# Transposing v and y of a delta-rule recurrence in whole 128x128 pieces instead of 64x64 ones

## The chip, the cores and the metric

The kernel runs on one core of one Trainium2 chip. The metric is the device time of one execution in microseconds (us). Engines go by the names that the profile gives them: PE (matrix products), PEld (its weight loads), DVE, ACT and POOL (elementwise work), SP (which issues most transfers).

## What is computed

One transformer-like block over 2048 tokens of width 1024: a modulated input projection, a gated MLP branch, a recurrent branch, a gated merge, an output projection with a layer norm, and a feed-forward layer of 4096 hidden features with a second layer norm. All is float32. The recurrent branch is what the change touches. Cut to that, the reference reads:

```python
def step(state, inp):            # 8 heads of 64 features, one state of 64x64 for each
    rt, wt, kt, vt, at, bt = inp
    sa = jnp.einsum('bhij,bhj->bhi', state, at)
    state = state * wt[:, :, None, :] + sa[..., None] * bt[:, :, None, :] + vt[..., None] * kt[:, :, None, :]
    yt = jnp.einsum('bhij,bhj->bhi', state, rt)
    return state, yt
...
y = (y - mu) * lax.rsqrt(var + GN_EPS) * gn_gain + gn_bias      # mu, var over the 64 features of a head
return (y + bonus) * g
```

## The kernel before, in words

The 2048 tokens are taken in four blocks of 512. A product with a float32 weight is made of three float32r products of 128x512 each (`mm3`, lines 461 to 463), because every operand is split into a rounded upper part and a rest (`split`: a rounding copy on ACT at line 395, a subtraction on DVE at line 396). These products fill PE nearly all the time. They come from `fm` (tiles `fm_ps`), from the feed-forward layer (`ff`, `pf`), from the output projection (`ops`) and from `uv` (`vps`).

The recurrent branch of a block runs between these products. `weave` (line 203) takes one step of the products (six of them, mostly) and lets the branch put its next part into PE's stream after as many steps as its last `yield` asked for. PE's order is thus written out by hand (`ORDERED`); the order on DVE, ACT, POOL and SP is made by a scheduler. A block's branch goes in four groups of 128 tokens, each of two chunks of 64: 16 groups in all. `rwkv_a` prepares the factors of a group, `rwkv_b` inverts its triangular matrices, and `rwkv_c` runs the recurrence over its two chunks.

`rwkv_c` is where the change lies. The features of two heads lie on the 128 partitions: head 0 of a pair on the lower 64 (`E`), head 1 on the upper 64 (`O`); there are `NP` = 4 pairs. `zq[:, p, 2]` holds v of pair p for the 128 tokens.

- At the start, v is turned so that tokens lie on partitions. For each chunk, head and pair, one 64x64 piece goes through `turn` (line 174), onto the half of the partitions that the head doesn't occupy. A piece from the lower half is made as an ordinary product with the identity (line 180 serves `rows.start == 0`, and each such product is two instructions in the trace), one from the upper half as a transposing instruction (line 178). Per group that is 16 pieces into two PSUM tiles `vt`; for each chunk ACT copies one half into `Q[O, 0]` (line 751) and DVE the other into `Q[E, 1]` (line 752).
- Then each chunk makes the tiles `xy` and `us` (lines 769 to 790), and its output leaves `xy` by a copy on ACT (line 793) and one on DVE (line 794) into `Yt`, with each head on its own half of the partitions.
- The group norm works on `Yt` (lines 796 to 805). Eight steps of products later, pair by pair with one step between, y is turned back: four 64x64 pieces by `turn` into `yp[:, 0]`, followed by the gate's product of 96x128 (line 813, two instructions in the trace) into `yp[:, 1]`. ACT and DVE take `yp` from there (lines 815 to 817).

Of the kernel before, what the change touches and what calls it, by code (L numbers as in the profile page):

```python
# [8 lines left out]
F32 = mybir.dt.float32  # L9
# [7 lines left out]
P = 128  # L17
# [6 lines left out]
C = 64  # L24
NC = HB // C
GW = 512
RW = 512
NP = 4
# [5 lines left out]
HC = 4  # L34
ORDERED = {mybir.EngineType.PE}
# how many steps of the products each part of the work between them stays behind, and a factor for each block
# [28 lines left out]
# weight tiles fetched ahead; first FF tiles that start under the transposes, and their lag  # L65
# [3 lines left out]
# the engine (a: ACT, v: DVE) that rounds the upper parts  # L69
# [20 lines left out]
class Body:  # L90
# [15 lines left out]
    # ---------------------------------------------------------------- setup  # L106
# [67 lines left out]
    def turn(self, out, x, rows):  # L174
        """transpose onto the other half of the partitions; the transposing form writes the lower half only"""
        ident = self.ident[rows, rows]
        if rows.start:
            self.nc.tensor.transpose(out, x, ident)
        else:
            self.nc.tensor.matmul(out, lhsT=x, rhs=ident, start=True, stop=True)  # L180

# [21 lines left out]
    def weave(self, gen, bg, drain=True):  # L203
        """bg yields how many steps of gen its next part should stay behind"""
        due = 0.0
        for _ in gen:
            due -= 1.0
            while due <= 0.0:
                w = next(bg, None)
                if w is None:  # L210
                    due = 1e9
                else:
                    due += w * self.lat
        if drain:
            self.go(bg)
# [5 lines left out]
    def setup(self):  # L221
# [5 lines left out]
        # masks over (s, t): strict t > s and inclusive t >= s, on both halves of the partitions  # L227
# [16 lines left out]
        # unit columns of the forward substitution: row i of lane group q is column 4 i + q  # L244
# [7 lines left out]
        # the two heads' indicators, and ones on the two heads' blocks  # L252
# [9 lines left out]
        # per-feature constants  # L262
# [11 lines left out]
        # 1 - mu and (1 - mu) bias  # L274
# [5 lines left out]
        # state  # L280
# [6 lines left out]
        # modulation: mod = silu(c) @ w_ada + b_ada, features on partitions  # L287
# [8 lines left out]
    def spatial_bias(self, wsT, spB, ones):  # L296
        """b_ln_v times the spatial weights' sums over s, + b_spatial, features on partitions"""
# [11 lines left out]
    def first_tiles(self):  # L309
        """the first projections of block 0, input tile by input tile as their modulation arrives"""  # L310
# [21 lines left out]
    def setup2(self):  # L332
        """the rest of the modulation"""
# [5 lines left out]
        # half of gt1 (the sigmoids are kept as 1 + tanh) and gt1 * b_out, along the free axis  # L339
# [6 lines left out]
    def setup3(self):  # L346
# [7 lines left out]
        # h2 = xhat * (g1 (1+sc2)) + (b1 (1+sc2) + sh2);  residual = xhat * (alpha g1) + (alpha b1 + gt2 b_ff2)  # L354
# [8 lines left out]
    def load_silu(self, pool):  # L363
        """2 silu(c) on every partition"""
# [7 lines left out]
    def load_ws(self, wsT):  # L372
        """[s, g, t], kept where t >= s"""
# [14 lines left out]
    # ------------------------------------------------------------ helpers  # L388
    def split(self, src, hi, lo, eng=None):
        """hi = src rounded to float32r, lo = src - hi: their products carry float32's digits"""  # L390
# [7 lines left out]
    def order(self):  # L398
        """the weight tiles in the order in which the projections take them"""
# [41 lines left out]
    def weights(self, n=D):  # L441
        """the next weight tile; those after it are fetched ahead"""
# [22 lines left out]
    def fm(self, xs, m=P, kt=KT, koff=0, each=None):  # L465
        """[m features, 512 tokens] = weights^T x, x feature-major in two parts"""
# [41 lines left out]
    def shift_mix(self, ps, m, name, i, c, out):  # L508
        """out = (1 - mu) z + mu (z of the token before), z = ps + bias"""
# [36 lines left out]
    # --------------------------------------------------------------- rwkv  # L546
# [15 lines left out]
    def rwkv_a(self, b, h, q):  # L562
# [26 lines left out]
        def first(p):  # L589
# [25 lines left out]
            # a~ = -k^ P(t-1), r~ = r P;  b~ = k^ a / P, k~ = k' / P  # L615
# [12 lines left out]
        def second(p, bk, kp):  # L628
# [13 lines left out]
            # bonus: (sum over the head of r k' r_k) v  # L642
# [11 lines left out]
        # squared norms of k^, one row for each head of a pair  # L654
# [4 lines left out]
        # 32 x 32 diagonal blocks and their norms, one for each lane; each lane group q solves 8 columns  # L659
# [12 lines left out]
    def rwkv_b(self, q):  # L672
# [16 lines left out]
        # T = (1 - L)^-1 diag(rn) by forward substitution  # L689
# [43 lines left out]
    def rwkv_c(self, b, h, q):  # L733
# [9 lines left out]
        Qs = []  # L743
        for c in range(NC):
            cs = slice(c * C, c * C + C)
            Q = rp.tile([P, 2, NP, C], F32, name="Q", tag="Q", bufs=2)
            vt = pst([P, 2, NP, C], "vt")
            for i in range(2):
                for p in range(NP):
                    self.turn(vt[half[1 - i], i, p], zq[half[i], p, 2, cs], half[i])  # L750
            nc.scalar.copy(out=Q[O, 0], in_=vt[O, 0])
            nc.vector.tensor_copy(out=Q[E, 1], in_=vt[E, 1])
            Qs.append(Q)
        # chunk by chunk
        Yt = rp.tile([P, NC, NP, C], F32, name="Yt", tag="Yt")
        for c in range(NC):
# [36 lines left out]
            nc.scalar.copy(out=Yt[O, c], in_=xy[O, 0])  # L793
            nc.vector.tensor_copy(out=Yt[E, c], in_=xy[E, 1])
        # group norm over each head, tokens on partitions
        yv = Yt.rearrange("p c h i -> p (c h) i")
# [11 lines left out]
        for p in range(NP):  # L808
            yp = pst([P, 2, HB], "yp")
            for i in range(2):  # L810
                for c in range(NC):
                    self.turn(yp[half[i], 0, c * C:c * C + C], Yt[half[1 - i], c, p], half[1 - i])
# [373 lines left out]
```

## Time and profile before

| | |
|---|---|
| median of 3 runs | 3162.5 us (3161.28 to 3165.88) |
| span of the profiled execution | 3158.4 us |
| instructions in the profile | 45776 |
| PE, DVE, ACT, POOL busy | 98%, 67%, 40%, 5% of the span |
| chain that ended last | PE 88%, DVE 6%, DMA 3%, ACT 1%, issue 1% |
| mean granted clock of PE | 0.996 of full speed |

The span runs from the first to the last instruction of the profiled execution, and it is the only time that the profile has of that execution. The median of the runs is 4.1 us (0.13%) above it. A busy share is an average over stages; which engine sets the pace in a stage is read from that stage's own rows. In a timeline, a row is one instruction, or several of one kind in a row (x4: four of them), with its start and how long it took from the start of the first to the end of the last. Matmuls overlap each other on PE, so the time that PE spends on one is the distance between starts, not its duration.

### The profile page before, as it was taken

The page shows a single profiled execution, that of the slowest core. Times are in us where ns is not written, and L with a number is a line of the kernel's source. Part 1 is how long each engine was busy: PE and PEld are TensorE (multiplying, and loading weights), DVE is VectorE, ACT ScalarE, POOL GpSimd, SP SyncE. Part 2 cuts the span into 40 slices and gives each one's busy share as a digit, 9 for nine tenths or more (in the row PEclk, how much of TensorE's full clock was granted, in tenths as well). Part 3 has the DMA queues.
Part 4 walks back from the last instruction along what each step waited for, and adds up shares of the span by engine and source line. Part 5 has one row for each costly group of instructions (what it writes and reads, how often), then busy time and mean ns, then how long its engine had stood idle before and what let it go on. Part 6 is the DMA issues. An engine that isn't in the chain of part 4 may idle for free.

```text
span 3158.4 us, 45776 instructions
## 1 busy us (share of the span) xinstructions
PE 3105.3 (98%) x17072; PEld 2485.8 (79%) x17072; DVE 2126.4 (67%) x4727; ACT 1267.9 (40%) x2012; POOL 143.8 (5%) x370
## 2 busy tenths in 40 slices
PE   8999999999999999999999999999999999999998
PEld 6776778777777877878777888787877788888887
DVE  7877873778777676586676557567668655854445
ACT  5524433353433334434433343453434334253332
POOL 1101100000000000100000000110000000000000
PEclk9999999999999999999999999999999999999999
DMA  8465544823323266444232245544333234623332
GB/s 286 152 177 162 171 144 144 279 90 85 103 77 93 81 198 200 140 135 123 92 96 84 87 138 192 174 120 155 105 97 91 83 87 134 230 87 96 98 97 97
DMA packets 241487, 416.78 MB, mean 132 GB/s; under 512 B 72465, under 2 KB 127377, under 8 KB 241265
## 3 DMA queue, kind: packets, MB, share of 16 engines
q1 hardware_dynamic: 241184, 413.59, 42.4%
q8 instruction: 135, 2.21, 0.3%
q14 instruction: 88, 0.71, 0.1%
q0 software_dynamic: 80, 0.26, 0.0%
HBM read 357.60 MB, written 56.17 MB: 131 GB/s over the span
## 4 chain that ended last, share of the span: by engine, by line
PE 88%; DVE 6%; DMA 3%; ACT 1%; issue 1%; SPq 0%; POOL 0%; DVEq 0%; ACTq 0%
PE fm_ps L461 15%; PE fm_ps L463 14%; PE fm_ps L462 14%; PE ff L461 7%; PE ff L462 7%; PE ff L463 7%; PE xy L769 2%; PE ops L462 1%; PE ops L463 1%; PE ops L461 1%; PE s L633 1%; PE vps L461 1%; PE vps L463 1%; PE vps L462 1%; PE us L778 1%; PE us L784 1%
## 5 line engine op out<-in xcount | busy, mean ns | idle before, releaser
L395 ACT CAST whi<-wraw 128x1024 fp32r<-128x1024 f32 (+1 forms) x500 | 494.9, 991 | 924.2 <-PE fm_ps L462 457.7
L396 DVE TENSOR_TENSOR wlo<-wraw,whi 128x1024 fp32r<-128x1024 f32 (+1 forms) x500 | 573.6, 1149 | 355.4 <-ACT whi L395 347.1
L461 PE MATMUL fm_ps<-xh,whi 128*128 128x512 f32 x1984 | 795.7, 401 | 2.9 <-ACT xh L395 2.3
L462 PE MATMUL fm_ps<-xl,whi 128*128 128x512 f32 x1984 | 774.2, 390 | 2.8 <-DVE xl L396 2.8
L463 PE MATMUL fm_ps<-xh,wlo 128*128 128x512 f32 x1984 | 775.0, 391 | 0.6 <-DVE wlo L396 0.6
L461 PEld LDWEIGHTS fm_ps<-xh,whi 128*128 128x128 f32 x1984 | 370.6, 187 | 91.6 <-issue 4.7
L463 PEld LDWEIGHTS fm_ps<-xh,wlo 128*128 128x128 f32 x1984 | 370.6, 187 | 83.1 <-DVE wlo L396 1.4
L462 PEld LDWEIGHTS fm_ps<-xl,whi 128*128 128x128 f32 x1984 | 371.1, 187 | 78.2 <-DVE xl L396 5.5
L461 PE MATMUL ff<-hh,whi 128*128 128x512 f32 (+1 forms) x1056 | 416.1, 394 | 0.7 <-ACT hh L395 0.7
L462 PE MATMUL ff<-hl,whi 128*128 128x512 f32 (+1 forms) x1056 | 404.9, 383 | 0.3 <-DVE hl L396 0.3
L463 PE MATMUL ff<-hh,wlo 128*128 128x512 f32 (+1 forms) x1056 | 404.7, 383 | 0.0
L1063 DVE SCALAR_TENSOR_TENSOR zr<-ff,mod,zr 128x512 f32<-128x512 f32 (+1 forms) x264 | 184.8, 731 | 149.4 <-PE ff L463 149.1
L461 PEld LDWEIGHTS ff<-hh,whi 128*128 128x128 f32 x1056 | 198.6, 188 | 45.4 <-issue 6.0
L463 PEld LDWEIGHTS ff<-hh,wlo 128*128 128x128 f32 x1056 | 198.5, 188 | 39.9
L462 PEld LDWEIGHTS ff<-hl,whi 128*128 128x128 f32 x1056 | 198.7, 188 | 35.8 <-DVE hl L396 0.5
L695 DVE TENSOR_TENSOR tmp<-T,L 128x4 f32<-128x4 f32 (+23 forms) x496 | 162.5, 328 | 10.4
L696 DVE TENSOR_REDUCE T<-tmp 128x1 f32<-128x4 f32 (+23 forms) x496 | 123.5, 249 | 10.3
L396 DVE TENSOR_TENSOR hl<-r,hh 128x512 fp32r<-128x512 f32 x128 | 87.9, 689 | 49.0 <-ACT hh L395 48.9
L462 PE MATMUL ops<-wlo,mh 128*128 128x512 f32 x256 | 101.2, 395 | 4.1 <-DVE wlo L396 4.1
L461 PE MATMUL ops<-whi,mh 128*128 128x512 f32 x256 | 101.3, 396 | 2.3 <-DVE ga L926 1.8
L462 PE MATMUL fm_ps<-yl,whi 128*128 128x512 f32 x256 | 102.1, 399 | 1.0 <-DVE yl L396 1.0
L461 PE MATMUL fm_ps<-yh,whi 128*128 128x512 f32 x256 | 102.7, 401 | 0.2 <-ACT yh L395 0.2
(240 smaller groups left out, 4099.9 us busy)
## 6 DMA issues: line engine op xcount, KB each, us to landing
wraw<-in_w_ff_dram SPq DMA_DIRECT2D x260, 512.0 KB
wraw<-in_w_gate_dram SPq DMA_DIRECT2D x64, 512.0 KB
wada<-in_w_ada_dram SPq DMA_DIRECT2D x48, 512.0 KB
wraw<-in_w_rkv_dram SPq DMA_DIRECT2D x42, 512.0 KB
gd<-g SPq DMA_DIRECT2D x64, 256.0 KB
ga<-gd SPq DMA_DIRECT2D x64, 256.0 KB
wraw<-in_w_out_dram SPq DMA_DIRECT2D x32, 512.0 KB
zd<-zmix SPq DMA_DIRECT2D x48, 256.0 KB
```

Of the source, the lines that this page charges most:

```text
L395: nc.scalar.copy(out=hi, in_=src)
L396: nc.vector.tensor_sub(lo, src, hi.bitcast(F32))
L461: nc.tensor.matmul(ps, lhsT=wh, rhs=xh, start=start, stop=False)
L462: nc.tensor.matmul(ps, lhsT=wh, rhs=xl, start=False, stop=False)
L463: nc.tensor.matmul(ps, lhsT=wl, rhs=xh, start=False, stop=stop)
L633: nc.tensor.matmul(sc[:, c], lhsT=bk[half[i], c], rhs=G[i][half[i], p, c], start=True, stop=True)
L695: nc.vector.tensor_mul(tmp[:, :n, :w], T[:, :n, :w], L[:, :w, t][:, None, :].to_broadcast([P, n, w]))
L696: nc.vector.tensor_reduce(T[:, :n, t:t + 1], tmp[:, :n, :w], axis=AX.X, op=ALU.add)
L769: nc.tensor.matmul(xy[:, i, p], lhsT=G[i][:, p, c], rhs=Q[:, i, p], start=(i == 0 and p == 0), stop=False, skip_group_check=True)
L778: nc.tensor.matmul(us[r, 0, p], lhsT=TT[r, p * NC + c], rhs=Xs[r, p], start=True, stop=True)
L784: nc.tensor.matmul(us[half[i], 1, p], lhsT=BK[:, p, c, half[i]], rhs=Q[:, i, p], start=True, stop=True)
L1063: self.nc.vector.scalar_tensor_tensor(res[:, n, ts], pfs[i], self.mod[:, 40 + n:41 + n], res[:, n, ts], op0=ALU.mult, op1=ALU.add)
```

## The change

For each group, v of a pair is turned in one transposing instruction of 128x128 instead of four pieces of 64x64. The result holds both chunks on the two halves of the partitions and both heads side by side, in one tile `vt` instead of two. The copies out of it, still two per chunk and of 64x256 elements each, take chunk c from its half and write the half where `Q` wants it, so for some the partitions that are read are not those that are written. `Yt` is laid out in the same way: token on the partitions, the two heads of a pair side by side; the copies out of `xy` write the half of their chunk, in four stretches of 64 elements. Then y of a pair is turned back by one transposing instruction of 128x128. `turn` is gone. The group norm, the gate's product, all other products, the DMAs and the numbers in the `yield`s stay. (The rest of the diff takes comments out.)

```diff
-        Qs = []
-        for c in range(NC):
-            cs = slice(c * C, c * C + C)
-            Q = rp.tile([P, 2, NP, C], F32, name="Q", tag="Q", bufs=2)
-            vt = pst([P, 2, NP, C], "vt")
-            for i in range(2):
-                for p in range(NP):
-                    self.turn(vt[half[1 - i], i, p], zq[half[i], p, 2, cs], half[i])
-            nc.scalar.copy(out=Q[O, 0], in_=vt[O, 0])
-            nc.vector.tensor_copy(out=Q[E, 1], in_=vt[E, 1])
-            Qs.append(Q)
-        Yt = rp.tile([P, NC, NP, C], F32, name="Yt", tag="Yt")
+        vt = pst([P, NP, 2, C], "vt")
+        for p in range(NP):
+            nc.tensor.transpose(vt[:, p], zq[:, p, 2], self.ident)
+        Qs = [rp.tile([P, 2, NP, C], F32, name="Q", tag="Q", bufs=2) for c in range(NC)]
+        for c in range(NC):
+            nc.scalar.copy(out=Qs[c][O, 0], in_=vt[half[c], :, 0])
+            nc.vector.tensor_copy(out=Qs[c][E, 1], in_=vt[half[c], :, 1])
+        Yt = rp.tile([P, NP, 2, C], F32, name="Yt", tag="Yt")
...
-            nc.scalar.copy(out=Yt[O, c], in_=xy[O, 0])
-            nc.vector.tensor_copy(out=Yt[E, c], in_=xy[E, 1])
-        yv = Yt.rearrange("p c h i -> p (c h) i")
+            nc.scalar.copy(out=Yt[half[c], :, 0], in_=xy[O, 0])
+            nc.vector.tensor_copy(out=Yt[half[c], :, 1], in_=xy[E, 1])
+        yv = Yt.rearrange("p k h i -> p (k h) i")
...
             yp = pst([P, 2, HB], "yp")
-            for i in range(2):
-                for c in range(NC):
-                    self.turn(yp[half[i], 0, c * C:c * C + C], Yt[half[1 - i], c, p], half[1 - i])
+            nc.tensor.transpose(yp[:, 0], Yt[:, p], self.ident)
             nc.tensor.matmul(yp[:, 1], lhsT=self.gup[:, p * P:p * P + P], rhs=xg, start=True, stop=True)
```

How the instructions stand on PE where v of the first group is turned, between the products of block 0's gates, before the change:

```order
L463 MATMUL fm_ps<-xh_153,wlo 128x512
L180 MATMUL vt<-ident,zq 64x64 x4
L178 MATMUL vt<-ident,zq 64x64 x4
L180 MATMUL vt<-ident,zq 64x64 x4
L178 MATMUL vt<-ident,zq 64x64 x4
L461 MATMUL fm_ps<-xh_154,whi 128x512
L462 MATMUL fm_ps<-xl_162,whi 128x512
```

And with it (lines have moved up by 8 here, and by 12 at the end of `rwkv_c`):

```order
L455 MATMUL fm_ps<-xh_153,wlo 128x512
L738 MATMUL vt<-ident,zq 128x128 x4
L453 MATMUL fm_ps<-xh_154,whi 128x512
L454 MATMUL fm_ps<-xl_162,whi 128x512
L455 MATMUL fm_ps<-xh_154,wlo 128x512
```

Sixteen pieces of two kinds have become four instructions of one kind, between the same two products.

On PE where y of the first pair of the first group is turned back, before:

```order
L463 MATMUL fm_ps<-xh_155,wlo 128x512
L178 MATMUL yp<-ident,Yt 64x64 x2
L180 MATMUL yp<-ident,Yt 64x64 x2
L813 MATMUL yp<-xg,gup 128x128
L461 MATMUL fm_ps<-xh_148,whi 128x512
L462 MATMUL fm_ps<-xl_156,whi 128x512
```

And with the change:

```order
L455 MATMUL fm_ps<-xh_155,wlo 128x512
L800 MATMUL yp<-ident,Yt 128x128
L801 MATMUL yp<-xg,gup 128x128
L453 MATMUL fm_ps<-xh_148,whi 128x512
L454 MATMUL fm_ps<-xl_156,whi 128x512
```

Four pieces have become one instruction, before the same product of the gate. The rest of PE's order is the same, instruction for instruction. On DVE, ACT, POOL and SP the scheduler has exchanged some neighbours, and no kind of instruction has become more or fewer.

On ACT, the copies out of `vt` of the first group wait for other engines as follows, before (a name in brackets is the engine that is waited for):

```order
L729 COPY TT<-tps 32x8x32 [waits DVE_49]
L751 COPY Q<-vt 64x256 [waits PE_49] x2
L891 ACTIVATE g<-fm_ps,hv 128x512 [waits DMAHW0_49,PE_49,Activation_49]
```

And with the change:

```order
L721 COPY TT<-tps 32x8x32 [waits DVE_49]
L741 COPY Q<-vt 64x256 [waits PE_49]
L741 COPY Q<-vt 64x256 [waits DVE_49]
L879 ACTIVATE g<-fm_ps,hv 128x512 [waits DMAHW0_49,PE_49,Activation_49]
```

The second copy on ACT, which waited for PE, now waits for DVE's copy out of the same tile.

## Rows read from the trace of the kernel before

**Rows 1.** The page, part 1: busy time, share of the span, instructions of an engine.

```profile
PE 3105.3 (98%) x17072; PEld 2485.8 (79%) x17072; DVE 2126.4 (67%) x4727; ACT 1267.9 (40%) x2012; POOL 143.8 (5%) x370
```

**Rows 2.** The page, part 4: the chain that ended last, by engine.

```profile
PE 88%; DVE 6%; DMA 3%; ACT 1%; issue 1%; SPq 0%; POOL 0%; DVEq 0%; ACTq 0%
```

**Rows 3.** Waits on PE, longest and one other: us in total, times, longest.

```profile
PE first L461 <- ACT xh L395: 12.9, 1, 12.9
...
PE yp L178 <- DVE Yt L805: 1.2, 1, 1.2
```

**Rows 4.** Windows A:B: length, busy time by engine, PE clock, DMA share, GB/s.

```profile
290.00:445.00 155.00, 154.74 (x1031) 120.86 (x1031) 123.89 (x334) 65.47 (x115) 21.47 (x43) 1.00 0.52 155
...
690.00:1140.00 450.00, 448.79 (x2733) 353.86 (x2732) 340.74 (x865) 173.59 (x309) 14.84 (x39) 1.00 0.32 96
...
2260.00:2640.00 380.00, 380.00 (x2275) 302.90 (x2274) 248.81 (x554) 151.57 (x251) 9.93 (x22) 1.00 0.31 92
```

**Rows 5.** Timeline, first group's v: start, us, engine, line, operation.

```profile
202.87 0.39 PE L463 MATMUL fm_ps<-xh,wlo 128*128 128x512 f32 x1
...
203.18 0.68 PE L180 MATMUL vt<-ident,zq 64*64 64x64 f32 x8
...
204.24 0.37 ACT L751 COPY Q<-vt 64x256 f32<-64x256 f32 x1 [1.72 <-PE vt L178]
204.64 0.42 DVE L752 COPY Q<-vt 64x256 f32<-64x256 f32 x1 [2.52 <-ACT Q L751]
...
205.07 0.50 PE L461 MATMUL fm_ps<-xh,whi 128*128 128x512 f32 x1
...
205.41 0.40 PE L462 MATMUL fm_ps<-xl,whi 128*128 128x512 f32 x1
```

**Rows 6.** Tiles vt and Q: count, duration ns min/median/max, first and last start.

```profile
L751 ACT COPY Q<-vt x32: 367/368/370, 204.2 to 2577.6; 64x256 f32<-64x256 f32 x32
...
L769 PE MATMUL xy<-Q,G x512: 217/275/294, 207.9 to 2599.1; 128*128 128x64 f32 x171
```

**Rows 7.** Timeline of PE: four transposing instructions of 128x128 in block 1's second input.

```profile
1479.30 0.40 PE L463 MATMUL pf<-xh,wlo 128*128 128x512 f32 x1
1479.53 0.60 PE L1012 MATMUL tp<-ident,zr 128*128 128x128 f32 x4
1479.89 0.47 PE L461 MATMUL pf<-xh,whi 128*128 128x512 f32 x1
1480.20 0.39 PE L462 MATMUL pf<-xl,whi 128*128 128x512 f32 x1
```

**Rows 8.** Timeline of PE, first group's second pair of y.

```profile
247.13 0.39 PE L463 MATMUL fm_ps<-xh,wlo 128*128 128x512 f32 x1
247.44 0.30 PE L178 MATMUL yp<-ident,Yt 64*64 64x64 f32 x2
...
248.05 0.49 PE L813 MATMUL yp<-xg,gup 96*128 96x128 f32 x2
248.29 0.48 PE L461 MATMUL fm_ps<-xh,whi 128*128 128x512 f32 x1
248.61 0.40 PE L462 MATMUL fm_ps<-xl,whi 128*128 128x512 f32 x1
```

**Rows 9.** Tile yp, the gate's product, as in rows 6.

```profile
L813 PE MATMUL yp<-xg,gup x128: 275/326/377, 245.7 to 2632.3; 96*128 96x128 f32 x128
```

**Rows 10.** Line 1012, the transposing instruction of 128x128, as in rows 6.

```profile
L1012 PE MATMUL tp<-ident,zr x128: 270/273/421, 659.0 to 2798.4; 128*128 128x128 f32 x128
```

**Rows 11.** Windows, as in rows 4: after a stall, and around eight transposing instructions.

```profile
1143.00:1148.00 5.00, 4.34 (x12) 3.46 (x13) 5.00 (x10) 0.62 (x1) 0.00 (x0) 0.66 0.46 157
...
1161.00:1166.00 5.00, 5.00 (x28) 4.20 (x27) 4.71 (x10) 1.40 (x3) 0.23 (x1) 1.00 0.91 287
```

**Rows 12.** Timeline of PE in the first of these windows.

```profile
1144.66 0.63 PE L461 MATMUL fm_ps<-yh,whi 128*128 128x512 f32 x1
...
1146.37 0.63 PE L462 MATMUL fm_ps<-yl,whi 128*128 128x512 f32 x1
```

More of the change, by code (lines that the diff above doesn't have):

```diff
@@ L172, in run @@
         left.close()
[L174 to L180, printed above, removed]
     def par(self, *gens):
```

## The prediction

> **What bounds the kernel now.** I read the shares first: PE is busy for 3105.3 of 3158.4 us, DVE for 67% of the span [rows 1]. That alone could be an average over unlike stages. So I read the chain that ended last, 88% of which is PE [rows 2], and then the waits: PE's longest single one is 12.9 us in the start-up, and at the pieces that the change replaces it is one of 1.2 us, before y is turned [rows 3]. Last come the stages in which the recurrent branch runs: PE is busy for 154.74 of 155 us, for 448.79 of 450 and for 380.00 of 380 [rows 4]. In these stages PE takes its instructions in the order written for it and waits for almost nothing. An instruction taken out there shortens the span by the step that it takes in PE's stream, as long as no other engine is caught up with.
>
> **The change part by part.** Costs are distances between starts in PE's stream: from the last product before a piece of work to the second product after it, because the first product after one is started early and pays for it in the next step.
>
> *v.* Between the products, the first group's v takes from 202.87 to 205.41, that is 2.54 us [rows 5]. The trace has the new work in another place: four transposing instructions of 128x128 between two products take from 1479.30 to 1480.20, 0.90 us, with the same two product steps in it [rows 7]. The difference is 1.64 us for a group. ACT copies out of `vt` 32 times, two for a group, so there are 16 groups [rows 6]: **16 x 1.64 = 26.2 us**.
>
> *y.* A pair of y takes from 247.13 to 248.61, 1.48 us; of this, 0.56 us lie behind the start of the gate's product at 248.05 [rows 8] and stay. In front of it, now 0.92 us, one transposing instruction comes instead: 0.23 us from the product to it (1479.30 to 1479.53) and one step of it. From the first of four to the product behind them it is 0.36 us; the last step, into that product, is the early start that I spoke of, some 0.03 us, so the three steps between the four are 0.33 / 3 = 0.11 us each [rows 7]. That makes 0.23 + 0.11 + 0.56 = 0.90 us, 0.58 us less. The gate's product has 128 instructions, two for a pair, so there are 64 pairs [rows 9]: **64 x 0.58 = 37.1 us**.
>
> *The step from a transposing instruction into the gate's product* stands nowhere in the trace. From below, it is as short as the step from one into a 128x512 product, 0.03 us, which gives another 64 x 0.08 = 5.1 us. From above, it takes the extra that the pieces show when PE goes from a full product to a 64-row piece: 0.31 us (202.87 to 203.18) against 0.23, some 0.08 us [rows 5, 7], which takes 64 x 0.08 = 5.1 us away. I keep 0.11 in the middle: the product of 96 rows leaves for a full one without such an extra (248.29 to 248.61, 0.32, against 0.31 after a transposing instruction) [rows 7, 8].
>
> Of the same transposing instruction the duration is 273 ns [rows 10], more than twice its step. The Trainium skill (TensorE: Matmul & The Clock Gate, Part 4: PE-mode transpose) gives about 275 ns for a 128x128 one in a kernel, and the trace agrees on the duration. If it meant the step, v would save 1.64 - 4 x 0.165 = 0.98 us for a group and y 0.58 - 0.165 = 0.41 us for a pair, 42 us in all by this estimate, and the time would be 3120; the steps of 0.11 us speak against it.
>
> *The copies.* There are as many as before, of as many elements; at 0.37 us on ACT and 0.42 on DVE [rows 5] they lie beside PE's products. They read one half of the partitions and may write the other, which no row shows; it may cost nothing, or, from above, double them, and neither reaches PE. What has changed is that all four of a group now wait for the one `vt` and go by turns, as ACT's second copy waits for DVE's first. Four in a row take 2 x 0.37 + 2 x 0.42 = 1.58 us, and some 0.1 us for handing over. They start when the last piece is through, about 203.10 + 3 x 0.11 + 0.27 = 203.7, and end near 205.4. PE wants the first two in `xy`, which stood at 207.9 [rows 6] and comes 1.64 us sooner, at 206.3. So there is 0.9 us left even for all four, and more for the two that are needed; were this cover gone, PE would wait what is missing, and 0.5 us in each of 16 groups would be 8 us. Behind the waiting copies on ACT and DVE stand the rounding and splitting of the next weights; they are held up by 0.4 us at a time, and DVE and ACT have idle time to make it up: in the stage where DVE is busiest it is 31 us of 155 [rows 4]. One PSUM tile less is taken for each group, which I cost at nothing: PE didn't wait for one here.
>
> *Everything else* on PE is in the same order. DVE, ACT, POOL and SP do the same work with some neighbours exchanged.
>
> **The sum.** 26.2 + 37.1 = 63.3 us off the span of 3158.4, 3095.1. The runs' median lies 4.1 us above the span, so 3099 is the same sum for a run. Each group becomes 1.64 + 4 x 0.58 = 4.0 us shorter for PE, while the transfers and DVE steps of the branch run beside it take as long as before; I allow a microsecond or two for new waits and forecast **3100 us**, 2.0% below 3162.5. A measurement of this kernel can tell about 0.2%, 6 us, from no change.
>
> **The rivals.**
>
> *DVE catches up with PE.* In a stretch of the first block DVE is busy for 123.89 of 155 us, 80%, in the second for 340.74 of 450, 76%; late in the kernel it is 248.81 of 380, 65% [rows 4]. If the eight groups of the first two stages (half of the 16) gave nothing because splits of weights come late, 31.7 us would be left: 3131 us. For it: DVE's queue is in order, with waits for ACT and DMA in it. Against it: the 450 us of the second stage hold the four groups of block 1, so 16 us less of it lifts DVE's share only to 340.74 / 434, 79%; by the same share of time saved, 80% would become some 83%. Short crowds on DVE that cost a few us are likelier than all of it.
>
> *The pieces were hidden, or the change does nothing for PE.* If pieces of 64x64 ran beside neighbouring products, removing them would free nothing and the time would be 3162. Against it: the distance between the products around them grows by their whole length, 2.54 us against the two steps of 0.23 that are left without them [rows 5].
>
> *The clock falls, and the kernel is slower.* PE's granted clock is 1.00 in the stages above [rows 4]. In 5 us around a stall it is 0.66 in the mean [rows 11], as it is at the lower of its two levels, 1.2 GHz, for a part of them; there, four product steps take from 1144.66 to 1146.37, 0.43 us each instead of 0.23 [rows 12]. If a transposing instruction did not count as work for the clock, each of the 16 + 64 places that now have nothing else could set off such a stretch. With the six products of one step behind each place at the lower level, that is 6 x 0.20 = 1.2 us a place and 80 x 1.2 = 96 us in all, against 63 us saved: 3195 us. It decides from 63 / 1.2 = 53 of the 80 places on; below that the kernel is still not slower. Against it: around a row of eight such instructions, twice what v has, the clock stays at 1.00 [rows 11], and here they lie between products. The Trainium skill (TensorE: Matmul & The Clock Gate, Part 4: PE-mode transpose) says that the full clock does not engage for this mode, as it doesn't count as activity of PE in the same way; by that rule this rival would be the forecast, and the row at 1.00 doesn't bear it out where products stand on both sides.
>
> **How the numbers follow.** The forecast with its own bounds, 3092 to 3112 (the step into the gate's product 5 us either way, waits of up to 8 us): 0.82. DVE catching up in part or in whole, 3112 to 3135: 0.12. No change that can be told: 0.02. The clock, or a wait of that size that I don't see, slower: 0.04. Faster is 0.82 + 0.12 = 0.94. To hold the time 8 times in 10 with room for a mis-sized term, the range goes from 3088 (the lower bound, and a few of PE's present waits gone) to 3125 (most of the second case).
>
> **What would show it.** In the profile after: 64 transposing instructions of v and 64 of y with a step of 0.11 us between those that follow each other; 0.90 us between the products around v, and the same around a pair of y; PE's busy time some 60 us less at the same share of 98%; no new wait at `xy` above 1 us; copies out of `vt` on ACT and DVE of 0.37 and 0.42 us, in turn. A clock under 0.99 in the mean, a PE that waits for `wlo` or `xl` from DVE in the first two stages, or a step into the gate's product of 0.2 us or more would prove steps of this wrong.

## The result, and the profile after

The changed kernel takes **3108.5 us** in the median of 4 runs (3107.61 to 3111.15), the kernel before 3162.6 beside it on the same chip (3161.28 to 3165.88): a ratio of 0.9831, 95% interval 0.9819 to 0.9842, so 54 us or 1.7% faster. The forecast was 3100, its range 3088 to 3125.

The page after, parts 1 and 4 (against [rows 1, 2]):

```profile
span 3109.3 us, 44483 instructions
...
PE 3046.7 (98%) x16432; PEld 2455.4 (79%) x16432; DVE 2124.0 (68%) x4727; ACT 1263.4 (41%) x2012; POOL 149.2 (5%) x370
...
PE 85%; DVE 9%; DMA 4%; issue 1%; ACT 1%; SPq 0%; POOL 0%; DVEq 0%; ACTq 0%
```

PE has 640 matmuls fewer and is busy for 58.6 us less. The time in which it isn't busy has grown, from 3158.4 - 3105.3 = 53.1 us to 3109.3 - 3046.7 = 62.6. DVE's share of the chain has gone from 6% to 9%.

The tiles after (count, duration ns min/median/max, first and last start):

```profile
L738 PE MATMUL vt<-ident,zq x64: 270/272/273, 203.8 to 2531.0; 128*128 128x128 f32 x64
L741 ACT COPY Q<-vt x32: 364/366/369, 204.4 to 2532.2; 64x256 f32<-64x256 f32 x32
L742 DVE COPY Q<-vt x32: 407/421/427, 204.8 to 2532.6; 64x256 f32<-64x256 f32 x32
...
L801 PE MATMUL yp<-xg,gup x128: 273/273/275, 243.4 to 2583.2; 96*128 96x128 f32 x128
L800 PE MATMUL yp<-ident,Yt x64: 270/271/332, 243.3 to 2583.0; 128*128 128x128 f32 x64
...
L759 PE MATMUL xy<-Q,G x512: 217/275/323, 207.0 to 2552.7; 128*128 128x64 f32 x171
```

There are 64 transposing instructions of v and 64 of y. The copies that read one half of the partitions and write the other cost no more than before: 366 ns against 368 on ACT [rows 6], 421 on DVE against the one of 0.42 us in [rows 5]. The last of the gate's products starts at 2583.2, where it started at 2632.3 before [rows 9].

The timeline after, around the first group's v and its second pair of y (start, us, engine, line, operation):

```profile
203.56 0.39 PE L455 MATMUL fm_ps<-xh,wlo 128*128 128x512 f32 x1
...
203.79 0.60 PE L738 MATMUL vt<-ident,zq 128*128 128x128 f32 x4
...
204.14 0.48 PE L453 MATMUL fm_ps<-xh,whi 128*128 128x512 f32 x1
...
204.42 0.36 ACT L741 COPY Q<-vt 64x256 f32<-64x256 f32 x1 [1.21 <-PE vt L738]
204.46 0.40 PE L454 MATMUL fm_ps<-xl,whi 128*128 128x512 f32 x1
...
204.82 0.42 DVE L742 COPY Q<-vt 64x256 f32<-64x256 f32 x1 [2.01 <-ACT Q L741]
...
205.27 0.37 ACT L741 COPY Q<-vt 64x256 f32<-64x256 f32 x1 [0.48 <-DVE Q L742]
...
246.50 0.39 PE L455 MATMUL fm_ps<-xh,wlo 128*128 128x512 f32 x1
246.73 0.27 PE L800 MATMUL yp<-ident,Yt 128*128 128x128 f32 x1
246.84 0.38 PE L801 MATMUL yp<-xg,gup 96*128 96x128 f32 x2
246.98 0.48 PE L453 MATMUL fm_ps<-xh,whi 128*128 128x512 f32 x1
247.30 0.39 PE L454 MATMUL fm_ps<-xl,whi 128*128 128x512 f32 x1
```

v takes 203.56 to 204.46, 0.90 us, as forecast, and the same in all 16 groups. A pair of y takes 246.50 to 247.30, **0.80 us, not 0.90**. The step into the gate's product is 0.11 us, the value taken. What the prediction let stay was the 0.56 us behind that product's start; now it is 247.30 - 246.84 = 0.46. From the start of the gate's two instructions to the next product took 0.24 us behind 64x64 pieces [rows 8] and takes 0.14 behind a whole transposing instruction. The copies out of `vt` go by turns, as forecast.

So what PE itself was spared is 16 x 1.64 + 64 x 0.68 = **69.7 us**, 6.4 more than forecast; the profiled executions differ by 49.1. About 20 us were given back. A first sight of where (windows after, columns as in [rows 4]):

```profile
290.00:445.00 155.00, 153.18 (x977) 120.81 (x976) 125.48 (x341) 65.05 (x114) 23.92 (x42) 0.98 0.51 156
...
690.00:1140.00 450.00, 443.79 (x2616) 353.44 (x2615) 352.59 (x883) 175.68 (x312) 15.69 (x39) 1.00 0.32 101
...
2260.00:2600.00 340.00, 340.00 (x1984) 274.68 (x1983) 233.59 (x527) 134.19 (x226) 8.61 (x19) 1.00 0.32 102
```

In the late stage PE still waits for nothing. In the first two windows it now has idle time, 1.8 of 155 us and 6.2 of 450, where it had 0.3 and 1.2 [rows 4]; and in the first of them the clock is at 0.98 instead of 1.00. The second window doesn't hold quite the same work in both kernels: 3.0 of the 6.2 us come after 1115, in block 1's merge, which before begins only at 1135.

The waits of PE after (us in all, times, longest):

```profile
PE ops L454 <- DVE wlo L388: 5.4, 2, 2.8
...
PE fm_ps L455 <- DVE wlo L388: 2.6, 3, 1.3
...
PE ua L587 <- issue: 2.0, 1, 2.0
PE tps L719 <- DVE Zs L715: 1.7, 1, 1.7
```

Before, the first two stood at 4.1 (longest 2.5) and 1.3, and `ua` and `tps` had none. Nothing new waits at `xy`; the 1.2 us before y [rows 3] are down to 0.3. Each wait is short, and DVE is behind nearly all of them; behind the one for `ua` too. By the times, its PSUM tile came free with DVE's line 805, the last step on a pair of y, and ahead of that step stands one of DVE's products for the modulation (tile `wada`):

```profile
250.29 1.22 DVE L376 SCALAR_TENSOR_TENSOR wada<-wada,siluB 128x1024 f32<-128x1024 f32 x1
...
251.95 0.28 DVE L805 TENSOR_TENSOR yb<-yp,y 128x128 f32<-128x128 f32 x1
...
252.34 0.46 PE L587 MATMUL ua<-xwa,lora 64*128 64x128 f32 x2 [2.02 <-issue]
```

DVE had been busy without a gap since 248.8. Before, the same instructions stood in the same order, but PE needed longer for its pairs of y, came later and didn't wait:

```profile
252.03 1.22 DVE L384 SCALAR_TENSOR_TENSOR wada<-wada,siluB 128x1024 f32<-128x1024 f32 x1
...
254.64 0.49 PE L595 MATMUL ua<-xwa,lora 64*128 64x128 f32 x2
```

What a wait costs is more than its length. The timeline of PE after, in the output projection of block 1 (a number in brackets is idle time before the row, and its releaser):

```profile
1194.66 0.40 PE L453 MATMUL ops<-whi,mh 128*128 128x512 f32 x1
1197.85 0.80 PE L454 MATMUL ops<-wlo,mh 128*128 128x512 f32 x1 [2.79 <-DVE wlo L388]
1198.44 0.63 PE L455 MATMUL ops<-whi,ml 128*128 128x512 f32 x1
...
1203.99 0.43 PE L453 MATMUL ops<-whi,mh 128*128 128x512 f32 x1
```

And at the same two instructions before:

```profile
1213.98 0.40 PE L461 MATMUL ops<-whi,mh 128*128 128x512 f32 x1
1216.02 0.50 PE L462 MATMUL ops<-wlo,mh 128*128 128x512 f32 x1 [1.64 <-DVE wlo L396]
1216.35 0.39 PE L463 MATMUL ops<-whi,ml 128*128 128x512 f32 x1
```

The wait for `wlo` was there before, 1.64 us long, with products at 0.23 us a step behind it. Now it is 2.79 us: PE is 19.3 us earlier at the product ahead of it, `wlo` only 18.2. And 13 steps of 0.43 us follow (1198.44 to 1203.99), where the granted clock is 0.50, the lower of its two levels, 1.2 GHz: 1.15 us more of waiting, and 13 x 0.20 = 2.6 us more for the products. In the whole execution I count 53 steps of 0.40 to 0.46 us from one 128x512 product to the next after and 16 before (16 more in each, one behind every product into `ssp`, are the same before and after and left out). The 37 more cost 7.4 us; with the 9.5 us of idle time that makes 16.9 of the 20.6 given back. Of these steps 12 and 7 lie in the start-up, ahead of the change's first instruction. All stretches of such steps after the start-up stand behind an idle PE, none behind a transposing instruction.

How the gain runs through the program can be read at one instruction: the first of twelve transposing instructions of block 1's second input, after nine groups of v and 32 pairs of y. Before:

```profile
1474.28 1.47 PE L1012 MATMUL tp<-ident,zr 128*128 128x128 f32 x12
```

After:

```profile
1457.37 1.47 PE L1000 MATMUL tp<-ident,zr 128*128 128x128 f32 x12
```

Up to there 16.9 us are gained, of 9 x 1.64 + 32 x 0.68 = 36.5 that PE was spared. From there to the last instruction of the same tile, which stands at 2798.4 before [rows 10] and at 2749.4 after, it is 49.0 - 16.9 = 32.1 of 33.2. **The loss lies in blocks 0 and 1, up to the output projection of block 1.** Taken at more of PE's instructions that stand in both traces, 9.7 us are missing where the merge of block 0 begins (566.5 before, 558.7 after), 12.2 at block 0's second input, 15.4 where the merge of block 1 begins, 19.6 behind block 1's output projection, and 20.6 at the end.

### The profile page after: what moved, and what is told of

It is laid out like the page before. It is cut to its first block, busy times and chain, and to the rows that moved or that the text cites. A ratio compares the mean times of both kernels' runs of the same rounds, so it can differ in the third digit from the quotient of the medians.

```text
span 3109.3 us, 44483 instructions
## 1 busy us (share of the span) xinstructions
PE 3046.7 (98%) x16432; PEld 2455.4 (79%) x16432; DVE 2124.0 (68%) x4727; ACT 1263.4 (41%) x2012; POOL 149.2 (5%) x370
## 4 chain that ended last, share of the span: by engine, by line
PE 85%; DVE 9%; DMA 4%; issue 1%; ACT 1%; SPq 0%; POOL 0%; DVEq 0%; ACTq 0%
PE fm_ps L453 15%; PE fm_ps L455 14%; PE fm_ps L454 14%; PE ff L453 7%; PE ff L454 7%; PE ff L455 7%; PE xy L759 2%; DVE wlo L388 1%; PE ops L454 1%; PE ops L455 1%; PE ops L453 1%; DVE tmp L687 1%; PE s L625 1%; PE vps L453 1%; PE us L768 1%
## 5 line engine op out<-in xcount | busy, mean ns | idle before, releaser
L455 PE MATMUL fm_ps<-yh,wlo 128*128 128x512 f32 x256 | 101.5, 397 | 2.0 <-DVE wlo L388 2.0
```

Source lines behind the costliest of these rows:

```text
L455: nc.tensor.matmul(ps, lhsT=wl, rhs=xh, start=False, stop=stop)
```

## The experiments

The theory was that PE's stream gets shorter by the steps counted, and that blocks 0 and 1 give some of it back. For that I had two explanations. *A:* PE comes earlier than DVE can follow in blocks 0 and 1, block 0 above all, in whose steps and merge DVE also makes 32 products for the modulation (`mods`, tile `wada`, 1.22 us each; the last one at 594 us). *B:* the scheduler's exchange of neighbours has put single instructions later on DVE, where 164 of 4727 stand elsewhere than before. A rival to the whole was that the transposing mode, and not the size of the pieces, brings the gain or takes it back, by the clock.

The first four kernels and the last four have four runs each; the kernel before took 3163.5 us beside the first four and 3161.6 beside the last. The four in between, without the modulation and with DVE in the program's order, have one run each (the kernel before: 3168.0). "The mark" is the instruction at 1474.28 above.

**One half of the change each.** The first keeps the pieces of y and its layout, the second those of v:

```diff
# e1: v only                                   # e2: y only
+nc.tensor.transpose(vt[:, p], zq[:, p, 2], self.ident)
                                               +nc.tensor.transpose(yp[:, 0], Yt[:, p], self.ident)
```

> The changed turning of v alone; y is turned in 64x64 pieces as before. PE's stream should lose 16 x 1.65 = 26.3 us against the kernel before. Theory A (crowds of DVE work in the first two blocks take back part of what PE gains there): the eight groups of the last two blocks give all of their 13.2 us, those of the first two only part of theirs, so 16 to 24 us are gained, 3139 to 3147 us. Theory B (only the scheduler's exchanged neighbours on DVE take time back): any value up to 26 us, 3136 us, without a pattern by block. If the two halves of the change add up, this kernel and the one with y alone together gain some 54 us.

> The changed turning of y alone; v is turned in 64x64 pieces as before. In the trace of the changed kernel a pair of y costs PE 0.35 us where it cost 1.03, so 64 x 0.68 = 43.5 us go from PE's stream. Theory A: the last two blocks give their 21.8 us, the first two only part of theirs, 30 to 40 us gained, 3122 to 3133 us. Theory B: up to 43 us, 3119 us, without a pattern by block. By the term of the prediction (0.58 us a pair) it would be 37 us at most.

v alone: 3136.1 us, ratio 0.9916 (0.99 to 0.9933), 27.4 us. y alone: 3131.8, ratio 0.9894 (0.9879 to 0.9908), 31.7 us. v's term of 26.2 is paid in full, against what A expected (16 to 24): its profile has gained 14.1 us at the mark (14.8 spared). y's is not, of 64 x 0.68 = 43.5: it has 6.3 of 21.8 at the mark, and after it 22.5 of 21.8. Together they give 59 us apart and 54 in one: what is given back is not proportional to what PE is spared. Nor does it follow the number of exchanges: by the traces 119 of DVE's instructions stand elsewhere than before with v alone, which loses nothing, and 35 with y alone, which loses 15.5 us up to the mark. So most of the loss comes with y.

**Ordinary products instead of the transposing mode**, of the same 128x128:

```diff
-            nc.tensor.transpose(vt[:, p], zq[:, p, 2], self.ident)
+            nc.tensor.matmul(vt[:, p], lhsT=zq[:, p, 2], rhs=self.ident, start=True, stop=True)
...
-            nc.tensor.transpose(yp[:, 0], Yt[:, p], self.ident)
+            nc.tensor.matmul(yp[:, 0], lhsT=Yt[:, p], rhs=self.ident, start=True, stop=True)
```

> The changed kernel with ordinary products of 128x128 with the identity in place of the transposing instructions, at both places. This parts the size of the pieces from the mode. An ordinary one is two instructions in the trace, of 0.21 and 0.11 us in the kernel before (the product with hones), 0.32 us against 0.11: 128 of them cost 128 x 0.21 = 27 us more on PE. If PE is the bound they show up but for what the crowds in the first two blocks hide: 15 to 27 us slower than the changed kernel, 3124 to 3136 us. If the transposing mode cost clock (the rival of the prediction), this kernel would have the higher mean clock and lose less, or even gain.

3111.9 us, ratio 0.9831 (0.9817 to 0.9846): as fast as the changed kernel, which I had not expected. PE does have more to do. Its timeline around the first group's v:

```profile
203.47 0.40 PE L455 MATMUL fm_ps<-xh,wlo 128*128 128x512 f32 x1
203.71 1.06 PE L738 MATMUL vt<-ident,zq 128*128 128x128 f32 x8
204.52 0.48 PE L453 MATMUL fm_ps<-xh,whi 128*128 128x512 f32 x1
204.84 0.39 PE L454 MATMUL fm_ps<-xl,whi 128*128 128x512 f32 x1
```

That is 1.37 us where the transposing mode takes 0.90; a pair of y takes 0.91 (246.13 to 247.04) instead of 0.80. PE is spared 16 x 1.17 + 64 x 0.57 = 55.2 us, 14.5 fewer. But it has 25.7 of its 28.8 at the mark, more than the changed kernel's 16.9, and 37 steps of 0.40 to 0.46 us instead of 53. So a later PE may find DVE done; but not by that alone, since the scheduler has made another order on DVE here (see the wait for `tps` below). The run shows that pieces of full size bring the gain in either mode, and that the mode's 14 us are within what DVE and the order decide. The mean clock is 0.996 here and 0.993 with the change; with the change the low stretches lie behind waits, so this difference is no sign of the mode.

**More room for the branch.** The numbers by which `weave` delays the branch's parts, 4% up:

```diff
-LAT0 = 1.05
-LAT1 = 1.0
+LAT0 = 1.09
+LAT1 = 1.04
```

> The changed kernel with the lags of the first two blocks 4% longer (LAT0 1.05 to 1.09, LAT1 1.0 to 1.04), so that the branch's parts come as late on PE, in time, as they did before the change. Theory A: part of the some 15 us that are missing in these blocks come back, 3 to 10 us, 3099 to 3106 us, unless the branch of block 0 then ends so late that the merge waits for it. Theory B: lags don't matter beyond a new exchange of neighbours, so within 3 us of the changed kernel, 3106 to 3112 us.

3123.5 us, ratio 0.9868 (0.9853 to 0.9883), some 14 us slower than the change. Its longest sum of waits is a new one:

```profile
PE fm_ps L453 <- ACT yh L387: 18.5, 9, 4.7
```

The branch now ends after the products that it lay beside, and the merge waits for it. Room can't be had for nothing: the wait is moved from the blocks to the merges.

**Without the modulation in block 0.** Both kernels leave out DVE's 32 products for the modulation in block 0's steps and merge, and with them the loads of `w_ada` that they read, 16 MB (the call that goes does both):

```diff
+        nc.vector.memset(self.mod[:, 16:48], 0.1)
...
-            self.mods([n])
```

> The kernel before, without the modulation's last 32 tiles (the loads of w_ada in setup2 and setup3 and the products with them on DVE, 1.2 us each, are left out; constants stand for their results). DVE has some 40 us less to do in block 0 and the first merge, and 16 MB are not loaded. It is the partner of the next one. PE is the bound, so it should be only some 5 to 15 us faster than the kernel before, by waits of PE that go, 3147 to 3158 us.

> The changed kernel with the same part of the modulation left out. Theory A (DVE is crowded in the first two blocks): with DVE lighter in block 0 the change should give nearly all of its 17.3 us there instead of 5 or 6, and 60 us or more in all against its partner. Theory B (an unlucky exchange of neighbours by the scheduler): the exchange is there also without the modulation, so the loss in the first two blocks stays near 15 us, and the change gives 49 to 54 us.

Before: 3164.9 us, after: 3094.9. The change is worth **70.0 us** here, the whole sum. The mark in the first and in the second:

```profile
1476.51 1.47 PE L1011 MATMUL tp<-ident,zr 128*128 128x128 f32 x12
...
1442.43 1.47 PE L999 MATMUL tp<-ident,zr 128*128 128x128 f32 x12
```

34.1 of 36.5 us are there, and 16.2 of 17.4 already where the merge of block 0 begins, where the change alone has 7.7. PE's wait for `ua` is gone. The order on DVE differs between these two kernels as well, for 142 of 4632 instructions, so an exchange of neighbours needn't cost anything. That speaks for A in block 0. It doesn't explain block 1, where no kernel makes a product for the modulation: from the end of block 0's second input to the mark the change lost 7.1 us, and this pair loses 1.2. And this pair has gained 4.1 us ahead of the first pair of y, where the first group's v accounts for 1.64. So some of the 70 us is luck. The time of the first was forecast at 3147 to 3158 and missed: without the modulation the kernel before got no faster. A new wait of 5.0 us for `zmix` from ACT stands in its trace (4.9 in that of the other), and what else kept it from the 10 us forecast I didn't look for.

**DVE in the order of the program** in both kernels, to take B's exchange out:

```diff
-ORDERED = {mybir.EngineType.PE}
+ORDERED = {mybir.EngineType.PE, mybir.EngineType.DVE}
```

> The kernel before with DVE's instructions in the order of the program too (ORDERED holds PE and DVE), so that the scheduler exchanges nothing there. It is the partner of the next one. As the order of the program puts whole parts of the branch ahead of the splits of weights, PE should wait for DVE more: 3165 to 3260 us.

> The changed kernel with DVE in the order of the program. DVE's instructions now stand in the same order in this kernel and in its partner. Theory B (only the scheduler's other order takes time back): the change gives its whole 69 us against the partner. Theory A (DVE has too little time in the first two blocks, whatever its order): the last two blocks give some 34 us, the first two clearly less than theirs, 45 to 60 us in all.

3526.0 and 3483.4 us, far above what I expected. In the first, PE waits for `wlo` 64 times in `fm_ps` alone, 126.8 us in all; the program's own order is a bad one for DVE. The change is worth 42.6 us in it. On DVE the two have one and the same order, instruction for instruction, and some 27 us are missing all the same: an exchange isn't needed for a loss. But as both kernels have long waits everywhere, and 42.6 us is below what A expected too (45 to 60), this doesn't tell how much of the change's own loss is A's and how much B's.

**The modulation off DVE:** POOL multiplies, ACT sums.

```diff
-            self.mods([n])
+            self.mods_off(n)
...
+        nc.gpsimd.tensor_tensor(out=w, in0=w, in1=self.siluB, op=ALU.mult)
+        nc.scalar.activation(w, w, AF.Identity, scale=0.5, accum_out=self.mod[:, n:n + 1])
+        nc.gpsimd.tensor_tensor(out=self.mod[:, n:n + 1], in0=self.mod[:, n:n + 1], in1=self.vec("b_ada", n), op=ALU.add)
```

> The changed kernel with all work kept, but the 32 later tiles of the modulation taken off DVE: POOL makes the product with silu(c), ACT sums it, POOL adds the bias. All loads of w_ada stay. Theory A with DVE as what is crowded: the time comes near that of the changed kernel without this modulation, 3094 us on a chip where the kernel before took 3168, so 3090 to 3100 us. If the loads of w_ada were what crowds the first block, not DVE, nothing comes back: 3105 to 3112 us. A wait for POOL, which is slower, could also make it lose in the first block.

> The kernel before with the modulation taken off DVE in the same way; the partner of the one above. PE set the pace in it already, so 3155 to 3166 us. The change should then be worth 62 to 70 us between the two, against 54 without this.

With the change 3138.8 us (ratio 0.9926, 0.9911 to 0.9941), without it 3199.4 (1.0121, 1.0102 to 1.014). The change is worth 60.5 us here, but both kernels have become slower, by 30 and 38 us. I had expected 3090 to 3112 for the first and 3155 to 3166 for the second. The trace of the first shows why DVE gained nothing. DVE has 32 products of 1.22 us less, 39 us, and yet is busy for 2128.6 us, against 2124.0 with them. Its timeline at one of POOL's products:

```profile
308.31 2.46 POOL L359 TENSOR_TENSOR wada<-wada,siluB 128x1024 f32<-128x1024 f32 x1
308.55 3.30 DVE L396 TENSOR_TENSOR wlo<-wraw,whi 128x1024 fp32r<-128x1024 f32 x1
```

DVE's subtraction starts 0.24 us after POOL's product and ends at 311.85, 1.08 us after it: its own 1.21 us begin about where POOL's product ends, and it took 3.30. The Trainium skill (SBUF — State Buffer, section Who interferes with whom) says that a DVE instruction with two inputs in SBUF contends with a GpSimd one that reads SBUF; the trace agrees, with 3.30 us. So DVE was no freer than before, and the pair settles nothing between DVE's load and the loads of `w_ada`. PE also waits for the new chain itself, 2.1 us once for POOL's line 361; what makes up the 30 and 38 us in all isn't shown.

**The small copies of the inverse on ACT.** PE's wait for `tps` points at one row. After the change, on DVE and PE:

```profile
391.23 0.74 DVE L509 SCALAR_TENSOR_TENSOR zmix<-zraw,vecs,zmix 128x512 f32<-128x512 f32 x1
...
394.18 0.42 DVE L715 COPY Zs<-zps 32x256 f32<-32x256 f32 x1
...
394.65 1.45 PE L719 MATMUL tps<-TT,Zs 32*32 32x32 f32 x32 [1.73 <-DVE Zs L715]
```

Between `zmix` and the copy DVE has nine small instructions (lines 606 to 615) that prepare factors in `rwkv_a`. Before, the copy came right behind `zmix`:

```profile
392.76 0.75 DVE L517 SCALAR_TENSOR_TENSOR zmix<-zraw,vecs,zmix 128x512 f32<-128x512 f32 x1
...
393.54 0.42 DVE L723 COPY Zs<-zps 32x256 f32<-32x256 f32 x1
```

This wait is the exchange's, theory B, and with it come 12 product steps of 0.43 us (396.62 to 401.74, granted clock 0.50). With ordinary products the copy stands right behind `zmix` again (391.92, `zmix` at 391.14), and with y alone too (393.69 and 392.92), so it is no part of what y alone loses. The edit takes both such copies off DVE:

```diff
-            (nc.scalar.copy if i else nc.vector.tensor_copy)(out=Zs[hi], in_=zps[hi])
+            nc.scalar.copy(out=Zs[hi], in_=zps[hi])
...
-            (nc.scalar.copy if i else nc.vector.tensor_copy)(out=TT[lo, :, 32:64], in_=tps[lo])
+            nc.scalar.copy(out=TT[lo, :, 32:64], in_=tps[lo])
```

> The changed kernel with both halves of Zs and of the last part of TT copied out of PSUM by ACT (before: one half by ACT, one by DVE). In the changed kernel one of these copies stands on DVE behind eight steps of the next pair, PE waits 1.8 us for it at 392 us, and the clock is low for 13 products after it, 4.8 us in all. This removes that one wait if nothing else moves: 3 to 6 us faster, 3102 to 3106 us. If the wait only goes elsewhere on DVE, no change.

3102.4 us, ratio 0.9807 (0.979 to 0.9823), **about 6 us less than with the change alone, and the fastest kernel here that leaves nothing out.** The intervals of the two ratios overlap a little (0.9819 is the lower end of the other), and the two kernels weren't run side by side, so the size of the step is uncertain. At the same place:

```profile
391.74 0.76 ACT L715 COPY Zs<-zps 32x256 f32<-32x256 f32 x2
...
393.08 1.09 PE L719 MATMUL tps<-TT,Zs 32*32 32x32 f32 x32
394.10 0.50 PE L453 MATMUL vps<-whi,xh 128*128 128x512 f32 x1
```

`tps` doesn't wait, and the next products run at full speed. At the mark this profile has 26.4 us instead of 16.9. Some 5 of the 9.5 us arise at this place, between the gate's products of the second and the third group; the rest arises later, without a cause shown. DVE's order has changed with the edit, too: the nine small instructions now stand behind a `wlo`, so the copy's move and the order aren't told apart.

> The changed kernel with both: the modulation off DVE and those copies on ACT. Theory A: 3088 to 3098 us, the fastest so far; no more than 3 us better than with the modulation alone, as the one wait is already gone there.

Both edits together: 3138.5 us, ratio 0.9925 (0.9904 to 0.9947), no better than the modulation on POOL alone, and 40 us above what I expected. That edit's loss covers the other's gain.

## Why the prediction was right, and where it was off

- *PE is the bound, and what leaves its stream shortens the time*: right where the other engines keep up. From the mark on, 32.1 of 33.2 us came through, and without the modulation in block 0 the whole 70, though some of that by luck.
- *v, 16 x 1.64*: right to the hundredth, 0.90 us around the four instructions; shown alone by the run with v only.
- *y, 64 x 0.58*: mis-sized. It is 0.68 a pair, 43.5 us instead of 37.1. The step into the gate's product was 0.11 us as taken; the failed step is "0.56 us lie behind the start of the gate's product ... and stay". It is 0.46. The extra behind a 64x64 piece was bounded for the instruction that comes next, but in the old rows it sat in the gate's own two instructions, which was read as theirs.
- *The 275 ns that the Trainium skill gives (TensorE: Matmul & The Clock Gate, Part 4: PE-mode transpose), read as a step*, from which 3120 followed: refuted, the steps are 0.11 us; as a duration it stands (270 to 273 ns).
- *The copies cost nothing*: right, in turn and at 0.37 and 0.42 us. `xy` starts at 207.0, not at 206.3, because v itself starts 0.6 us later (203.79 against 203.18), which lies ahead of the change's first instruction.
- *"A microsecond or two for new waits"*: the term that failed most. From the medians 69.7 - 54.1 = 15.6 us were given back. Two errors of opposite sign, +6.4 and about -15, left the forecast 8.5 us low: that it came so near is in part luck.
- *The rival "DVE catches up"* happened in part. It was priced at all of the first two stages' 31.7 us; about 20 of 36.5 went in the profiled execution. The argument against it was that DVE's share would only rise from 80% to 83% and from 76% to 79%. It did no more than that, to 81% and 78% (125.48 of 155, 352.59 of 450), and the loss came all the same: it is the kind of reading that the prediction itself warns of, as a share says nothing about one instruction that stands behind nine others on DVE. The sign it named, PE waiting for `wlo` or `xl` in the first two stages, is not there: in those windows PE waits for `Zs`, `T`, `kp` and `zr` of DVE and once for `yh` of ACT. The waits for `wlo` that have grown stand in the merge of block 0 (569.1 and 575.6) and in block 1's output projection.
- *The clock as a rival* is refuted as told: the 80 places set off nothing. The clock took part another way, behind the new waits, some 6 to 7 us.

Shown: that the loss is in blocks 0 and 1, that y alone brings most of it and v alone none, that it goes when block 0's modulation and its loads are left out, that one new wait (`ua`) stands behind a product of the modulation on DVE where DVE's order is that of before, and that another (`tps`) stands behind an exchange and goes, with about 6 us, when the two copies leave DVE. Open: whether DVE's work or the loads of `w_ada` make block 0 tight in the main, as the run meant for it was spoilt by POOL; what takes some 7 us in block 1, where there is no modulation; and what the rest of the exchange costs. A kernel after the change with the DVE order of the kernel before was not tried.

## What to carry to other kernels

Price an edit on a bound engine by distances between starts, from the instruction before the piece of work to the second one after it, and look at both sides of a switch between shapes: an extra that a small piece causes can sit in its successor's steps. On an engine that is busy for 98%, what leaves its stream is gained in full where the other engines have slack for each single hand-over; where they have not, it comes back as many waits of 1 to 3 us, and behind some of them as products at the lower clock, so price stages apart and give the tight ones a part of their share. Then read the new waits one by one: two copies moved to an engine with idle time gave back some 6 us.

## What the runs showed of the hardware that was not expected

- A wait of PE can cost more than its length: behind 2.79 us of idle time 13 product steps took 0.43 us instead of 0.23; behind 1.64 us at the same place before, none did. The length alone doesn't decide it: with the change, 12 such steps follow the 1.73 us before `tps` and none follow the 2.02 us before `ua`, where the granted clock stays at 1.00 (250 to 256).
- Four ordinary float32 products of 128x128, two instructions each, take 0.81 us to the start of the next product (203.71 to 204.52), four transposing instructions 0.35 (203.79 to 204.14); both are far below the sixteen pieces of 64x64, 1.89 us (203.18 to 205.07) [rows 5].
- A copy from PSUM that reads one half of the partitions and writes the other costs what one within a half costs, 366 ns on ACT and 421 on DVE.
- POOL holds up a subtraction of DVE that begins behind its own product until that product is about done, 3.30 us for 1.21 (308.55). One that began 0.14 us ahead of POOL's product (583.88, 128x512) took 0.68, and POOL's product 2.81 instead of 2.40.
